# Splitting six of the twelve matmuls of zeros at the head of a matmul-and-rotation kernel

## Chip, cores and metric

The kernel runs on one core of a Trainium2 chip. The metric is the device time of one execution in microseconds (us), as the median of several runs.

## The reference

`x` is 16 x 512 x 768, `weight` 768 x 768, `cos` and `sin` 512 x 64, all float32; there are 12 heads of 64 columns. The product is rotated in halves of each head:

```
y = np.matmul(x, weight).reshape(batch, seq, n_heads, head_dim)
y1, y2 = y[..., :32], y[..., 32:]
out1 = y1 * cos1 - y2 * sin1
out2 = y2 * cos2 + y1 * sin2
out = np.concatenate([out1, out2], axis=-1)
```

Here `cos1` and `sin1` are the first 32 columns of `cos` and `sin`, `cos2` and `sin2` the last 32, spread over batch and heads.

## The kernel before

The 8192 rows of `x` are cut into 64 tiles of 128 rows, four tiles to a group. A tile is loaded, cast to float16, transposed to bring the contraction onto the partitions, and multiplied with the weight, which is held in float16 in six chunks of 128 x 768 (indices 0 to 5). A product of 128 x 768 goes to six banks of 512 columns in PSUM (`py`). VectorE multiplies each stretch of a bank with cosines and sines (`rope`, line 446), GpSimd adds the two products (line 468), and the results are stored.

All instructions are written through one helper, `do`, which works out from the names read and written what each instruction must wait for, and puts it at the end of its engine's program. The order on each engine is thus the order of the calls.

The head of the program is written out by hand. SyncE issues the loads of tile 0 and 1, weight chunk 0, tile 2, weight chunks 1 and 2, tile 3, weight chunks 3 to 5, and then cosines and sines. VectorE first fills `cold` (128 x 512, float16) with zeros. TensorE's program begins with twelve matmuls of `cold` with itself, written by `warm`: nine (`warm(9)`), then the transposes of tile 0, then three more (`warm(3)`), then the transposes of tile 1. Each takes a load of 128 x 128 and streams 512 columns into one of the six banks in turn. The last six open the accumulation of the banks of group 0 with zeros, so that the true matmuls of that group (`mm0`) all add; the first six write zeros that these replace. Nothing waits for any of the twelve by a signal of its own (`tick=False`), but TensorE works in order.

After these come, in TensorE's order, chunk 0 with tiles 0 and 1 (line 340), the transposes of tile 2 (line 260), chunks 1 and 2 with tiles 0 and 1, then tile 2 with chunks 0 and 1, the transposes of tile 3, and so on through chunk 5; each chunk waits for its cast on VectorE (`cast_w`, line 194), and each transpose for the cast of its tile on ScalarE (`castx`, line 194). The transposed tiles 0 and 1 are copied out of PSUM by VectorE, ahead of the cast of chunk 0; later tiles are copied by ScalarE. When chunk 5 is cast, VectorE prepares the sines (lines 625 and 627) and starts on the products. From there on the work is a loop over tiles, with TensorE's matmuls in halves of 64 rows (line 365).

Of the kernel before, what the change touches and what calls it, by code (L numbers as in the profile page):

```python
# [16 lines left out]
class Flow:  # L17
# [24 lines left out]
    def do(self, e, make, reads=(), writes=(), dma=None, tick=True, after=0):  # L42
        need = {}
        for k in reads:
            for s, v in self.wrote.get(k, {}).items():
                need[s] = max(need.get(s, 0), v)
        for k in writes:
            for d in (self.wrote, self.readby):
                for s, v in d.get(k, {}).items():
                    need[s] = max(need.get(s, 0), v)  # L50
        if e == "pe":
            need.pop("pe", None)
            if after:
                need["pe"] = after
        waits = self.settle(e, need)
        for s, v in waits[:-1]:
            self.eng[e].wait_ge(self.sem(s), v)  # L57
        i = make(self.eng[e])
        if waits:
            s, v = waits[-1]  # L60
            i.wait_op(self.sem(s), v, "sem-ge")
        name, step = (dma, 16) if dma else (e, 1)
        self.sem(name)
        self.order[name] = len(self.order) + sum(self.count.values())
        at = self.count[name] + step
        if tick or dma:
            i.then_inc(self.sems[name], step)
            self.count[name] = at
            self.known[name, at] = dict(self.seen[e])
        for k in reads:  # L70
            d = self.readby.setdefault(k, {})
            d[name] = max(d.get(name, 0), at)
        for k in writes:
            self.wrote[k] = {name: at}
            self.readby[k] = {}
        return i
# [32 lines left out]
def kernel(  # L109
# [11 lines left out]
    f = Flow(nc, tc)  # L121
    do = f.do
    P = nc.NUM_PARTITIONS
# [25 lines left out]
    def sbuf(name, shape, dt):  # L149
        return nc.alloc_sbuf_tensor(name, shape, dt).ap()  # L150
# [4 lines left out]
    cold = sbuf("cold", [P, 512], FP16)  # L155
# [26 lines left out]
    py = nc.alloc_psum_tensor("py", [P, 6 * 512], FP32).ap()  # L182
# [322 lines left out]
    def store_half(g, h, c, at):  # L505
# [20 lines left out]
       reads=["ident"], writes=["ident32"])  # L526
# [49 lines left out]
    WARM = 12  # L576
    warmed = [0]

    def warm(k):
        for _ in range(k):  # L580
            b = warmed[0] % 6
            do("pe", lambda eng: eng.matmul(  # L582
                py[:, ts(b, 512)], cold[:, 0:P], cold, start=True, stop=warmed[0] < WARM - 6),
                reads=["cold"], writes=[f"ps{b}"], tick=False)
            warmed[0] += 1

    def mm0(i, c):
# [10 lines left out]

    U0 = units(0)
    warm(9)  # L600
    castx(0, "act")
    turn(0, "dve")
    castx(1, "act")
    warm(3)
    turn(1, "dve")
    castx(2, "act")
# [13 lines left out]
    for c in CHUNKS[3:5]:  # L620
# [8 lines left out]
        reads=["sin", "csn1", "cos"], writes=["csn"])  # L629
# [74 lines left out]
    for i in range(QB, NTILE):  # L704
# [17 lines left out]
        for n, p in enumerate(pieces(g, s)) if i >= ROWS else ():  # L722
# [3 lines left out]
            for c in CHUNKS:  # L726
                mm_piece(i, p, c, c == CHUNKS[0], c == CHUNKS[-1],
                         tick=c == CHUNKS[-1])
# [60 lines left out]
```

## Time and profile before

| | |
|---|---|
| three plain runs | 149.9, 150.1, 150.23 us; median 150.1 us |
| the profiled execution | 150.49 us, with a span of 148.6 us |
| TensorE matmuls (PE) | 140.1 us busy (94%), 1894 |
| TensorE weight loads (PEld) | 110.8 us (75%), 1894 |
| VectorE (DVE) | 127.6 us (86%) |
| ScalarE (ACT) | 75.9 us (51%) |
| GpSimd (POOL) | 123.4 us (83%) |
| the twelve matmuls of zeros (line 582) | 4.4 us busy, all before 6.4 us |

The profile is of one execution, and its times count from the start of the span. A record of a matmul lasts until its result is written, so records of neighbouring matmuls overlap; the pace is read from the distance of their starts. A weight load is a record of its own (PEld) and may run beside a matmul. The chain that ended last is followed back from the last instruction to what released each step.

### The profile page before, as it was taken

How to read it: one execution, taken by the hardware profiler on the slowest of the kernel's cores; microseconds unless marked ns; L12 is line 12 of the kernel's file. 1: busy time of each engine (PE TensorE's matmuls, PEld its weight loads, DVE VectorE, ACT ScalarE, POOL GpSimd, SP SyncE). 2: the span in 40 equal slices, each digit the busy share in tenths (PEclk: the TensorE clock that was granted, in tenths of full speed). 3: DMA queues.
4: the chain of work that ended last, by engine and by line, in shares of the span. 5: the costliest groups of instructions: out<-in, count | busy, mean ns of one | idle time of the engine just before them, and what ended most of it. 6: DMA issues, size and time to landing. Idle time of an engine off the chain costs nothing.

```text
span 148.6 us, 4352 instructions
## 1 busy us (share of the span) xinstructions
PE 140.1 (94%) x1894; PEld 110.8 (75%) x1894; DVE 127.6 (86%) x103; ACT 75.9 (51%) x87; POOL 123.4 (83%) x76
## 2 busy tenths in 40 slices
PE   6769999999999999999999999999999999999960
PEld 2325568888888888888888888888888888766850
DVE  0344998888989999999989998999989999999990
ACT  3444698888242924466262824465455839840010
POOL 2000389999999999999999999779899999899970
PEclk9999999999999999999999999999999999999998
DMA  4999999999999999999999999999999999998783
GB/s 127 352 395 405 400 402 272 249 330 329 331 331 328 333 329 332 342 392 332 327 339 394 360 329 331 382 391 395 391 399 405 396 398 392 400 406 354 275 314 116
DMA packets 36227, 51.28 MB, mean 345 GB/s; under 512 B 7664, under 2 KB 28912, under 8 KB 36208
## 3 DMA queue, kind: packets, MB, share of 16 engines
q1 hardware_dynamic: 16336, 28.05, 54.7%
q10 hardware_dynamic: 14432, 20.97, 38.2%
q0 software_dynamic: 5440, 1.97, 10.7%
q8 instruction: 15, 0.25, 0.6%
q14 instruction: 4, 0.03, 0.1%
HBM read 27.79 MB, written 25.17 MB: 356 GB/s over the span
## 4 chain that ended last, share of the span: by engine, by line
PE 77%; DVE 12%; DMA 5%; issue 2%; SPq 1%; DVEq 0%
PE py L365 68%; DVE tq L446 7%; DMA w_raw<-in_weight_dram 5%; PE py L340 4%; PE pt L275 4%; DVE w_raw L446 2%; SPq L214 1%; PE pt L260 1%; SPq L236 1%; DVE ov L415 1%; DVE py L408 0%; DVE xs L408 0%; DVE w_sb L194 0%; DVEq L57 0%; SPq L784 0%
## 5 line engine op out<-in xcount | busy, mean ns | idle before, releaser
L468 POOL TENSOR_TENSOR ov<-tq 128x512 f32<-128x512 f32 (+3 forms) x34 | 76.1, 2261 | 19.5 <-DVE tq L446 19.0
L446 DVE TENSOR_TENSOR tq<-py,csn 128x1024 f32<-128x1024 f32 (+2 forms) x51 | 74.4, 1495 | 3.8 <-PE py L365 2.9
L365 PE MATMUL py<-w_sb,xt 64*128 64x512 f16 (+1 forms) x768 | 73.8, 323 | 0.0
L365 PEld LDWEIGHTS py<-w_sb,xt 64*128 64x128 f16 x768 | 53.5, 94 | 10.6 <-DVE tq L446 0.4
L365 PE MATMUL py<-w_sb,xp 64*128 64x256 f16 (+1 forms) x528 | 52.1, 323 | 0.0
L194 ACT COPY xt<-pt 128x768 f16<-128x768 f16 x38 | 30.3, 801 | 38.6 <-PE pt L275 33.9
L194 ACT CAST xc<-xs 128x768 f16<-128x768 f32 x40 | 36.1, 907 | 18.8 <-PE py L365 7.4
L365 PEld LDWEIGHTS py<-w_sb,xp 64*128 64x128 f16 x528 | 37.1, 94 | 6.6
L446 DVE TENSOR_TENSOR w_raw<-py,csn 128x1024 f32<-128x1024 f32 (+1 forms) x22 | 35.3, 1604 | 2.8 <-PE py L365 2.4
L468 POOL TENSOR_TENSOR ov<-w_raw 128x1536 f32<-128x1536 f32 (+2 forms) x15 | 35.5, 2379 | 0.5 <-DVE w_raw L446 0.4
L340 PE MATMUL py<-w_sb,xt 128*128 128x256 f16 (+1 forms) x102 | 17.0, 317 | 1.6 <-DVE w_sb L194 1.3
L340 PEld LDWEIGHTS py<-w_sb,xt 128*128 128x128 f16 x102 | 9.2, 98 | 7.7 <-DVE w_sb L194 3.0
L275 PEld LDWEIGHTS pt<-ident,xc 64*128 64x128 f16 x408 | 13.2, 95 | 1.3 <-issue 0.2
L275 PE MATMUL pt<-ident,xc 64*128 64x64 f16 x408 | 13.0, 191 | 0.0
L229 POOL DMA_DIRECT2D xh<-in_x_dram x20 | 11.7, 592 | 0.0
L194 ACT CAST xd<-xb 128x1536 f16<-128x1536 f32 x7 | 11.5, 1637 | 0.0
L194 DVE CAST w_sb<-w_raw 128x768 f16<-128x768 f32 x6 | 3.4, 560 | 4.1 <-DMA w_raw<-in_weight_dram 4.0
L303 DVE STREAM_TRANSPOSE xp<-xd 128x768 f32<-128x768 f32 x7 | 6.8, 970 | 0.0
L303 DVE STREAM_TRANSPOSE xp<-xh 128x768 f32<-128x768 f32 x5 | 6.2, 1242 | 0.0
L582 PE MATMUL py<-cold 128*128 128x512 f16 x12 | 4.4, 525 | 1.4 <-DVE cold L519 1.4
L194 ACT COPY ov<-py 128x256 f32<-128x256 f32 x1 | 0.4, 372 | 10.0 <-PE py L478 10.0
L194 DVE COPY xt<-pt 128x768 f16<-128x768 f16 x2 | 1.1, 557 | 4.8 <-PE pt L260 4.8
(26 smaller groups left out, 22.6 us busy)
## 6 DMA issues: line engine op xcount, KB each, us to landing
out_dram<-ov ACTq DMA_DIRECT2D x53, 384.0 KB, 12.6
xs<-in_x_dram SPq DMA_DIRECT2D x40, 384.0 KB, 14.1
xb<-in_x_dram SPq DMA_DIRECT2D x28, 192.0 KB, 16.2
out_dram<-ov SPq DMA_DIRECT2D x4, 768.0 KB, 6.1
w_raw<-in_weight_dram SPq DMA_DIRECT2D x6, 384.0 KB, 7.5
xh<-in_x_dram POOLq DMA_DIRECT2D x20, 96.0 KB, 13.1
out_dram<-ov SPq DMA_DIRECT2D x1, 384.0 KB, 3.7
out_dram<-ov SPq DMA_DIRECT2D x3, 128.0 KB, 2.6
```

What stands on the lines that cost most here:

```text
L194: eng.copy(out=o, in_=i_) if e == "act" else eng.tensor_copy(out=o, in_=i_)
L214: do(e, lambda eng: eng.dma_start(out=xs_b[k], in_=x[b].rearrange("(p r) h -> r p h", r=SB)[r]), writes=[f"xs{k}"], dma=f"xs{k}")
L229: do(e, lambda eng: eng.dma_start(out=dst[ts(q, R)], in_=src[r, q]), writes=[f"{name}q{q}"], dma=name)
L236: do(e, lambda eng: eng.dma_start(out=w_raw[:, t, h], in_=wv[t, h]), writes=[f"wr{t}{h}"], dma=f"ov{t}_{1536 * (1 - h)}")
L260: do("pe", lambda eng: eng.transpose(pt[:, t, h, :], src[:, t, h, :], ident), reads=[f"xc{c}", "ident"], writes=[f"pt{k}"], tick=(t, h) == ...
L275: do("pe", lambda eng: eng.transpose(pts[r][:, t, h, :], src[rows, t, h, :], ident[rows, rows]), reads=[f"xc{c}", "ident"], writes=[f"pt{r ...
L303: do("dve", lambda eng: eng.transpose(out=dst, in_=src), reads=rd, writes=[f"xp{z}"])
L340: do("pe", lambda eng: eng.matmul(ps, get(t, h), w_sb[:, t, h, a - s * H : z - s * H], start=start, stop=stop), reads=[key, f"w{t}{h}"], w ...
L365: do("pe", lambda eng: eng.matmul(py[:, a:z], get(t, h)[rows], w_sb[rows, t, h, a - s * H : z - s * H], start=start, stop=not opens and en ...
L446: do("dve", lambda eng: eng.tensor_tensor(out=tq.rearrange("p j (h d) -> p j h d", d=D), in0=ps.rearrange("p (h d) -> p h d", d=D) .unsque ...
L468: do(adder, lambda eng: eng.tensor_tensor(out=ov_b[o][:, ds(c0, w)].rearrange("p (h t d) -> p h t d", t=2, d=HD), in0=tq[:, 0].rearrange(" ...
L582: do("pe", lambda eng: eng.matmul(py[:, ts(b, 512)], cold[:, 0:P], cold, start=True, stop=warmed[0] < WARM - 6), reads=["cold"], writes=[f ...
```

## The change

Of the twelve matmuls of zeros, the first six are each written as four: the same load of 128 x 128 zeros, and 128 columns streamed instead of 512, into the four quarters of the same bank. The last six stay as they are, and so does everything else. Since each matmul has its load, TensorE's program has 18 loads and 18 matmuls more.

```diff
     def warm(k):
         for _ in range(k):
             b = warmed[0] % 6
-            do("pe", lambda eng: eng.matmul(
-                py[:, ts(b, 512)], cold[:, 0:P], cold, start=True, stop=warmed[0] < WARM - 6),
-                reads=["cold"], writes=[f"ps{b}"], tick=False)
+            n = 128 if warmed[0] < WARM - 6 else 512
+            for c in range(0, 512, n):
+                do("pe", lambda eng: eng.matmul(
+                    py[:, ds(b * 512 + c, n)], cold[:, 0:P], cold[:, ds(c, n)],
+                    start=True, stop=warmed[0] < WARM - 6),
+                    reads=["cold"], writes=[f"ps{b}"], tick=False)
             warmed[0] += 1
```

## The prediction

> **What bounds the kernel now.** I read the page first, then the chain that ended last in order of time, then the timeline of the first 20 us, because the edit touches only TensorE's first instructions. The page gives the span and who carries the end:
>
> ```profile
> span 148.6 us, 4352 instructions
> ...
> ## 4 chain that ended last, share of the span: by engine, by line
> PE 77%; DVE 12%; DMA 5%; issue 2%; SPq 1%; DVEq 0%
> ```
>
> Three quarters of the chain is TensorE (PE), so an edit on TensorE could matter. But the share is an average; the question is where that chain enters TensorE. In order of time it does so here:
>
> ```profile
> 3.28 6.97 DMA w_raw<-in_weight_dram
> 10.25 0.02 issue
> 10.27 0.57 DVE w_sb L194
> 10.84 0.05 issue
> 10.89 1.47 PE py L340 x8
> ...
> 123.72 1.95 PE py L365 x17
> ```
>
> Before 10.89 us nothing on TensorE is on the chain. The end is set by the third chunk of the weight (index 2): its transfer takes 6.97 us from 3.28 and lands at 10.25, VectorE (DVE) casts it in 0.57 us, and only then does TensorE start a stretch that the chain follows nearly without a break to 125 us. The twelve matmuls of zeros lie wholly ahead of it. The timeline shows how they lie beside the real work (columns: start, duration, engine, line and operation; in brackets the idle time before and what ended it):
>
> ```profile
> 1.40 3.57 PE L582 MATMUL py<-cold 128*128 128x512 f16 x9 [1.40 <-DVE cold L519]
> 1.80 0.15 PEld L582 LDWEIGHTS py<-cold 128*128 128x128 f16 x1 [0.28 <-issue]
> ...
> 4.17 1.82 ACT L194 CAST xc<-xs 128x768 f16<-128x768 f32 x2 [1.98 <-DMA xs<-in_x_dram]
> ...
> 4.36 0.12 PEld L582 LDWEIGHTS py<-cold 128*128 128x128 f16 x1 [0.28 <-issue]
> 5.16 0.35 PEld L260 LDWEIGHTS pt<-ident,xc 128*128 128x128 f16 x6 [0.68 <-issue]
> 5.19 0.49 PE L260 MATMUL pt<-ident,xc 128*128 128x128 f16 x6 [0.22 <-ACT xc L194]
> ...
> 5.53 0.81 PE L582 MATMUL py<-cold 128*128 128x512 f16 x3
> 5.73 0.56 DVE L194 COPY xt<-pt 128x768 f16<-128x768 f16 x1 [4.38 <-PE pt L260]
> ...
> 6.17 0.50 PE L260 MATMUL pt<-ident,xc 128*128 128x128 f16 x6
> ...
> 6.71 0.56 DVE L194 COPY xt<-pt 128x768 f16<-128x768 f16 x1 [0.43 <-PE pt L260]
> ...
> 7.38 0.56 DVE L194 CAST w_sb<-w_raw 128x768 f16<-128x768 f32 x1
> ...
> 8.00 0.82 PE L340 MATMUL py<-w_sb,xt 128*128 128x512 f16 x4 [1.33 <-DVE w_sb L194]
> ...
> 9.27 0.51 PE L260 MATMUL pt<-ident,xc 128*128 128x128 f16 x6 [0.45 <-ACT xc L194]
> 9.30 0.56 DVE L194 CAST w_sb<-w_raw 128x768 f16<-128x768 f32 x1 [1.36 <-DMA w_raw<-in_weight_dram]
> ```
>
> Nine matmuls of zeros run from 1.40. Seven loads lie between 1.80 and 4.36 at equal steps, so one matmul of 512 columns takes (4.36 - 1.80)/6 = 0.427 us there. The three that start at 5.53 take 0.81 us together. With the shortest record of one, 0.379 (quoted next), that is (0.81 - 0.38)/2 = 0.215 us a step. TensorE therefore runs at half pace first and at full pace later. The change falls at about 4.38: the nine end at 1.40 + 3.57 = 4.97, less the 0.379 - 0.215 = 0.164 us by which a record outlasts its step, 4.81; the eighth, loaded at 4.36, and the ninth thus fit in 0.45 us, two steps at full pace and 0.02 us. The page's clock row does not show the half pace (its first slice is a 9, as all but the last are), so I go by the steps:
>
> ```profile
> PEclk9999999999999999999999999999999999999998
> ...
> L582 PEld LDWEIGHTS py<-cold x12: 97/132/151, 1.4 to 5.7; 128*128 128x128 f16 x12
> L582 PE MATMUL py<-cold x12: 379/607/635, 1.4 to 6.0; 128*128 128x512 f16 x12
> L260 PEld LDWEIGHTS pt<-ident,xc x36: 96/98/101, 5.2 to 18.1; 128*128 128x128 f16 x36
> L260 PE MATMUL pt<-ident,xc x36: 216/220/232, 5.2 to 18.1; 128*128 128x128 f16 x36
> ```
>
> These are the durations (minimum, median, maximum, in ns) of the zero matmuls and of the transposes. The transposes matter as a price, because their shape is exactly the new one: a load of 128x128 and a stream of 128 columns. Six take 0.50 us from 6.17; less the record of the last (0.22), that is (0.50 - 0.22)/5 = 0.056 us a pair at full pace. That is a quarter of 0.215, although each pair's own load record is 0.098 us: the loads hide behind the streams.
>
> **The change part by part.** It removes six pairs of load and 512-column matmul and adds 24 pairs of load and 128-column matmul: 18 loads and 18 matmuls more, on the same banks, with the same operand of zeros. It adds no wait: the first matmul still waits for the memset of zeros, none of the new ones signals, and the six that open the accumulation in the banks are as before.
>
> *Streaming time.* Columns stay the same: 6 x 512 = 24 x 128. At half pace a 128-column stream is 0.427/4 = 0.107 us, so 24 x 0.107 = 2.56 us against 6 x 0.427 = 2.56 us. Difference: 0.
>
> *The loads.* At half pace one load's record is 0.15 us, longer than the 0.107 us stream meant to hide it, and no row shows a 128-column matmul at half pace. So I bound it. Low end: hidden, as at full pace (0.098 us record, 0.056 us step); cost 0. It cannot be below zero, since the columns are the floor. High end: load and stream strictly one after the other. A pair then takes 0.107 + 0.15 = 0.257 us at half pace and 0.056 + 0.098 = 0.154 us at full pace. Between 1.40 and 4.38 (2.98 us) 11.6 pairs pass; the other 12.4 take 1.91 us, to 6.29; the three long ones end at 6.29 + 3 x 0.215 = 6.94, against 4.81 before. I take the low end, because its row is the same shape and both load and stream slow together.
>
> [...]
>
> *What that reaches.* What covers both ends is the wait for the weight. At the low end the nine end at 4.81 and the first transposes wait for ScalarE's cast until 5.19 anyway. At the high end everything follows in TensorE's order: transposes of tile 0 from 6.94 to 7.28, the last record outlasting its step by 0.16 more; three long matmuls to 7.92; transposes of tile 1 to 8.26, visible at 8.42; VectorE's copy (0.56) to 9.0, its cast of chunk 0 (0.56) to about 9.6; four matmuls of 1536 columns (3 x 0.215 = 0.65) to 10.28; transposes of tile 2 (0.33) to 10.61; chunk 1 (0.65) to 11.26. Chunk 2 then starts at 11.26 instead of 10.89, 0.37 late. What is next behind that?
>
> ```profile
> 14.81 1.74 PEld L340 LDWEIGHTS py<-w_sb,xt 128*128 128x128 f16 x12 [0.22 <-DVE w_sb L194]
> ...
> 15.28 0.23 DVE L627 TENSOR_SCALAR csn<-sin_sb 128x128 f32<-128x128 f32 x1
> 15.54 6.75 DVE L446 TENSOR_TENSOR tq<-py,csn 128x1024 f32<-128x1024 f32 x4
> ...
> 16.84 0.34 PEld L260 LDWEIGHTS pt<-ident,xc 128*128 128x128 f16 x6 [0.30 <-ACT xc L194]
> ...
> 19.30 0.56 PEld L365 LDWEIGHTS py<-w_sb,xt 64*128 64x128 f16 x7 [0.36 <-DVE tq L446]
> ```
>
> The first product on VectorE starts at 15.54, right after its own scaling of the sines. The matmul it needs starts at 14.81 and takes about 0.39, so it is there at 15.20: 0.34 us of slack. A shift of 0.37 moves VectorE by 0.03 us, and TensorE, which waits for VectorE at 19.30 and for ScalarE at 16.84, takes up the rest in those waits. So the sum is 0 at the low end and 0.03 us at the high end.
>
> *The pace.* The doubling at 4.38 could move. Earlier is worth nothing, since 5.19 is ScalarE's. Later: if the pace doubled only after tile 1's transposes, nine long matmuls' worth would end at 5.24, transposes (0.64) at 5.88, three long ones at 7.16, transposes at 7.80, visible at 7.96, copy and cast to 9.13, then at full pace 9.82, 10.15, 10.80: still ahead of 10.89. So up to about 7.8 us a late doubling is free too.
>
> The profiled execution took 150.49 us with its span of 148.6; the three plain runs have a median of 150.1, 0.39 below, from 149.9 to 150.23. A sum of 0 gives 150.49 there and 150.1 as the median. A measurement can tell about 0.2% here, 0.3 us.
>
> **The rivals.**
>
> *Slower: the small matmuls do not bring the pace up.* Suppose that only long matmuls in an unbroken stretch do, 2.98 us of them as before. Then three at 3.96 are followed by transposes at 5.24, three more break off at 7.16, and the next long stretch is chunk 0's, from 9.17. At half pace it takes 3 x 0.427 = 1.28 to 10.45, transposes to 11.09, and with the doubling at 9.17 + 2.98 = 12.15 chunk 1 ends at 12.26. Chunk 2 is 1.37 late, less 0.34 of slack: 1.03 us, which nothing later gives back as the chain stays on TensorE and VectorE; 151.1 us. It decides once chunk 2 starts after 10.89 + 0.34 = 11.23. Against it: the same columns stream without a gap at the low end, and the trace before shows the pace holding through idle time and transposes from 6.5 to 8.0. For it: no row shows the pace rising on short matmuls. [...]
>
> [...]
>
> *Faster: more loads bring the pace up sooner in executions in which it comes late.* The plain runs may differ in that from the profiled one. The gain is then at most what the late ones lose: from the median 150.1 to the fastest, 149.9, or a little below if all three lost something. Against it: a late doubling is free up to 7.8 us.
>
> **How the numbers follow.** No change gets 0.68, of which 0.02 strays over 0.2% on either side by scatter; the first slower rival 0.10 (151.1), the second 0.06 (151.4); the faster one 0.16 (149.9), half of it beyond 0.2%. Faster is 0.08 + 0.02 = 0.10, slower 0.10 + 0.06 + 0.02 = 0.18, the same 0.64 + 0.08 = 0.72. The forecast is 150.1. The plain runs spread over 0.33 us, so half of that, some 0.16, is what another set may stray. The range is the fastest run less that, 149.75, which takes in the faster rival, and the slowest plus that, the 0.03 us of the loads and a little of the rivals, 150.5; both slower rivals, 0.16 together, stay outside.
>
> **What would show it.** Right: 24 zero matmuls starting 0.107 us apart from 1.40, the nine old ones' place ending near 4.8, tile 0's transposes near 5.19 waiting for ScalarE, chunk 0 at 8.00, the chain entering TensorE near 10.89 from the weight's transfer. The load step is wrong if the starts are further apart than 0.107; that costs the end nothing unless chunk 2 slips past 11.23. The forecast is wrong if matmuls of 512 columns still step by 0.427 after 7.8 us, or if the chain enters TensorE through line 582.

## The result, and the profile after

The changed kernel took 149.81 us (median of 17 runs, 149.07 to 150.56) against 150.22 us (17 runs, 149.70 to 150.65). The ratio is 0.9961, with a 95% interval of 0.9944 to 0.9978: 0.39% faster, 0.22% to 0.56%. "The same" was forecast, at 150.1 us in a range from 149.75 to 150.5; the time lies in the range, but the gain is real and had been given 1 in 10. Ratios here leave out executions more than 1.5% above the fastest of their kernel, and they are not the ratio of the two medians, which differ here by 0.41 us (0.27%).

The head looks as forecast. The page's span and the chain in order of time, of after:

```profile
span 148.2 us, 4388 instructions
...
3.28 6.84 DMA w_raw<-in_weight_dram
10.12 0.02 issue
10.14 0.57 DVE w_sb L194
10.72 0.05 issue
10.76 1.47 PE py L340 x8
```

The chain still enters TensorE from the third weight chunk, 0.13 us earlier than before because the transfer took 6.84 us instead of 6.97. The timeline of after:

```profile
1.40 2.69 PEld L584 LDWEIGHTS py<-cold 128*128 128x128 f16 x26 [1.40 <-DVE cold L519]
1.40 4.02 PE L584 MATMUL py<-cold 128*128 128x128 f16 x27 [1.40 <-DVE cold L519]
...
5.29 0.80 PE L260 MATMUL pt<-ident,xc 128*128 128x128 f16 x6
5.88 1.10 PE L584 MATMUL py<-cold 128*128 128x512 f16 x3
...
7.83 0.55 DVE L194 CAST w_sb<-w_raw 128x768 f16<-128x768 f32 x1
```

The single starts in the trace (1.697, 1.804, 1.911 and so on) are 0.107 us apart, so the loads hide behind the streams at half pace too. TensorE doubled its pace later in this execution, about 6.5 us instead of 4.4: the transposes of tile 0 take 0.80 us here, 0.49 before. Chunk 0 is cast 0.45 us later and nothing follows from it.

So the gain of the profiled pair, 0.4 us of span, is not at the head. Nor is it in the long middle: VectorE's first product starts 0.15 us earlier (15.39 against 15.54), but that lead is lost at about 125 us (more on this below), and its last add ends within 0.07 us of before. The two rows are of the last add before and after:

```profile
144.13 0.42 DVE L415 TENSOR_TENSOR ov<-py,xs 128x256 f32<-128x256 f32 x1
```

```profile
144.19 0.42 DVE L415 TENSOR_TENSOR ov<-py,xs 128x256 f32<-128x256 f32 x1
```

It lies behind that: the last stores. Transfers from 139 to 149 us, first before, then after (queue, packets, MB, share; and per issue the size and the time from issue to landing):

```profile
q8 instruction: 1, 0.02, 0.5%
issues: line engine op xcount, KB each, median us to landing
out_dram<-ov SPq DMA_DIRECT2D x1, 384.0 KB, 3.7
out_dram<-ov ACTq DMA_DIRECT2D x1, 384.0 KB, 3.4
out_dram<-ov SPq DMA_DIRECT2D x3, 128.0 KB, 2.6
```

```profile
q10 hardware_dynamic: 288, 0.52, 14.0%
issues: line engine op xcount, KB each, median us to landing
out_dram<-ov SPq DMA_DIRECT2D x1, 384.0 KB, 2.3
out_dram<-ov ACTq DMA_DIRECT2D x1, 384.0 KB, 2.4
out_dram<-ov SPq DMA_DIRECT2D x3, 128.0 KB, 2.0
```

Before, one packet of the queue named "instruction" falls among the last stores, and all of them land later. After, there is none (the list of queues ends with q10). The last two half microseconds show what goes with it, before and after (the two columns at the end are the DMA share and GB/s):

```profile
146.00:146.50 0.50, 0.00 (x0) 0.00 (x0) 0.00 (x0) 0.00 (x0) 0.00 (x0) 1.00 0.61 203
146.50:147.00 0.50, 0.00 (x0) 0.00 (x0) 0.00 (x0) 0.00 (x0) 0.00 (x0) 1.00 0.05 16
```

```profile
146.00:146.50 0.50, 0.00 (x0) 0.00 (x0) 0.00 (x0) 0.00 (x0) 0.00 (x0) 0.91 0.70 230
146.50:147.00 0.50, 0.00 (x0) 0.00 (x0) 0.00 (x0) 0.00 (x0) 0.00 (x0) 0.50 0.00 0
```

A share of 0.05 is less than one engine of sixteen: a single DMA engine works on alone, and the end waits for it. The packets of the trace say the same: before, the last eight of 1,024 bytes start about 0.042 us apart, one behind the other with nothing beside them, and the last packet of all ends at 146.88.

I take the instruction packet for a fetch of TensorE's program. The page of before, like that of after, has the row

```profile
q8 instruction: 15, 0.25, 0.6%
```

By the trace these are 15 packets of 16,384 bytes each, for 3788 loads and matmuls; between two of them TensorE starts on average 246 loads and matmuls. The last packet starts at 141.69 us before (it is 0.88 us long) and at 137.96 after. Of the loads and matmuls, 3763 have started by then before and 3729 after. That is 34 fewer, and 36 of the 3729 are the new ones, so in the work that both kernels share the last fetch comes 70 records earlier. That the new ones moved it is what the experiments test; why by 70 and not by 36 stays open.

From this two theories. **A:** the gain comes because 36 more instructions ahead of the end move TensorE's last program fetch out of the last stores. **B:** the head did it, by short columns, more loads or the pace. What A speaks of is read within one execution: the time from the end of VectorE's last add to the end of the last store's packet, 2.33 us before and 1.84 after, is called the last stretch below.

### The profile page after: what moved, and what is told of

Same layout as the page of the kernel before. It is cut to its first block, busy times and chain, and to the rows that moved or that the text cites. A ratio compares the mean times of both kernels' runs of the same rounds, so it can differ in the third digit from the quotient of the medians.

```text
span 148.2 us, 4388 instructions
## 1 busy us (share of the span) xinstructions
PE 140.9 (95%) x1912; PEld 113.0 (76%) x1912; DVE 127.5 (86%) x103; ACT 75.9 (51%) x87; POOL 123.3 (83%) x76
## 4 chain that ended last, share of the span: by engine, by line
PE 77%; DVE 12%; DMA 5%; issue 2%; SPq 1%; DVEq 0%
PE py L365 68%; DVE tq L446 7%; DMA w_raw<-in_weight_dram 5%; PE py L340 5%; PE pt L275 4%; DVE w_raw L446 2%; SPq L214 1%; PE pt L260 1%; SPq L236 1%; DVE ov L415 1%; DVE py L408 0%; DVE xs L408 0%; DVE w_sb L194 0%; DVEq L57 0%; SPq L787 0%
## 5 line engine op out<-in xcount | busy, mean ns | idle before, releaser
L584 PE MATMUL py<-cold 128*128 128x128 f16 (+1 forms) x30 | 5.1, 363 | 1.4 <-DVE cold L519 1.4
```

The lines of the kernel that those rows point to most:

```text
L584: do("pe", lambda eng: eng.matmul(py[:, ds(b * 512 + c, n)], cold[:, 0:P], cold[:, ds(c, n)], start=True, stop=warmed[0] < WARM - 6), read ...
```

## The experiments

All but e9 and e12 are edits of the kernel before. A wait on a semaphore that is long met changes nothing in what is computed; two of them make one instruction (the trace of e1 has 36 more semaphore records on TensorE for its 72 waits, 53 against 17).

**e1, 36 instructions more at the head.**

```diff
     turn(1, "dve")
+    for _ in range(72):
+        nc.tensor.wait_ge(f.sem("dve"), 1)
```

> The kernel before, with its twelve zero matmuls of 512 columns, and 72 waits on an already met semaphore in TensorE's program behind the transposes of tile 1; two such waits make one instruction, so 36 instructions more, as many as the change added. Theory A (program fetch: 36 more instructions move the last 16 KB fetch of TensorE's program out of the last stores): that fetch starts near 138 us instead of 141.7, the last 384 KB store of SyncE lands in about 2.3 us instead of 3.7, and the time is 0.3 to 0.5 us below the kernel before. Theory B (short columns or more weight loads at the head, the pace of TensorE): no gain, within 0.15 us of before, fetch anywhere.

Measured: the last stretch was 1.82 us, as A says, but the time was 152.22 us, with a ratio of 1.0086 (1.0049 to 1.0123). The waits were dear, about 0.09 us an instruction (3.26 us over 36). The timeline of e1:

```profile
6.26 0.50 PE L260 MATMUL pt<-ident,xc 128*128 128x128 f16 x6
10.02 0.81 PE L340 MATMUL py<-w_sb,xt 128*128 128x512 f16 x4 [3.26 <-issue]
```

TensorE stood still for 3.26 us and began chunk 0 two microseconds late. The longest runs had the lowest granted clock (0.977 to 0.989, against 0.997 and 0.998 in the three shortest). The profiled execution, 150.83 us, is one of those three. The expected gain was missed, so e5 repeats the idea without waits.

**e2, the same at the end.** The 72 waits stand behind `for add in after_all + late: add()`.

> The kernel before, with the same 36 instructions more (72 met waits) behind the last matmul of TensorE's program instead of at its head. Theory A: what comes before the last fetch is not longer, so it stays near 141.7 us inside the last stores, and the time is within 0.15 us of before. If it were the sheer length of the program, wherever it is added, the gain of 0.4 us would be here too. Theory B: within 0.15 us of before.

Measured: the last fetch came at 142.09 us, the last stretch was 2.50 us, and the ratio 0.999 (0.9962 to 1.0017). The length of the program alone brings no gain that can be told.

**e3 and e4, one block more, and one block and 36.**

```diff
     for i in range(QB, NTILE):
         g, s = divmod(i, QB)
+        if 8 <= i < 56:
+            for _ in range(2 * ((i - 7) * spread // 48 - (i - 8) * spread // 48)):
+                nc.tensor.wait_ge(f.sem("dve"), 1)
```

with `spread` 256 in e3 and 292 in e4.

> The kernel before with 256 instructions more (512 met waits) spread evenly over the tiles 8 to 55: just one 16 KB block of TensorE's program (64 bytes each). Theory A: one fetch more in all (16), and the last again near 141.7 us inside the last stores: store landing about 3.7 us as before. If the waits are hidden by TensorE's queue the time is that of before, within 0.15 us; if not, it is longer by their cost, which the next kernel shares. Theory B says nothing of the fetch; no gain.

> The same with 292 instructions more (584 met waits), one block and 36. Theory A: the last fetch is again near 138 us, ahead of the last stores, which land in about 2.3 us; 0.3 to 0.5 us less than the kernel with 256 more. Theory B: no difference between the two but the cost of 36 waits, so the same or slower.

Measured: e3 has one fetch more, by its page:

```profile
q8 instruction: 16, 0.26, 0.6%
```

So the packets are TensorE's: 256 instructions added to its program bring one more. The last comes 2.94 us ahead of the end of VectorE's last add (2.86 before), and the last stretch is 2.24 us. By that a packet of 16,384 bytes holds about 256 instructions, some 64 bytes each; ahead of this run only the 246 loads and matmuls between two packets of before spoke for it. In e4 it comes 6.80 us ahead (6.66 in the change), and the last stretch is 1.84. That repeats, one block on, what A asks of the fetch and of the stretch. The times do not: 152.47 us (ratio 1.0140, 1.0110 to 1.0169) and 154.35 us (1.0259, 1.0230 to 1.0289). A had asked for 0.3 to 0.5 us less in e4 than in e3, and it took 1.9 us more, as theory B allows. The waits are not hidden, and the last 36 cost more than the tail gives, so these two say nothing for A on the total.

**e5, the change's 36 instructions as zeros elsewhere.**

```diff
     turn(1, "dve")
+    for j in range(18):
+        do("pe", lambda eng: eng.matmul(
+            py[:, ds(j % 6 * 512, 128)], cold[:, 0:P], cold[:, 0:128], start=False, stop=False),
+            reads=["cold"], writes=[f"ps{j % 6}"], tick=False)
```

> The kernel before with its twelve zero matmuls whole, and 18 more of 128 columns (18 loads and 18 matmuls, the change's 36 instructions) behind the transposes of tile 1, where TensorE has 1.3 us to wait; they add zeros to open banks. 18 x 0.056 = 1.0 us fits into that wait. Theory A (36 instructions more move TensorE's last program fetch ahead of the last stores): fetch near 138 to 139 us, the stretch from VectorE's last add to the last store's packet 1.8 us instead of 2.3, time 0.4 us below before, as with the change. Theory B (the head: short columns in place of long, or the pace): no gain, within 0.15 us.

Measured: the time was 149.91 us, with a ratio of 0.9960 (0.9933 to 0.9988); the last fetch came at 137.62, and the last stretch was 1.83. The transfers of e5, again from 139 to 149 us:

```profile
q10 hardware_dynamic: 288, 0.52, 14.1%
issues: line engine op xcount, KB each, median us to landing
out_dram<-ov SPq DMA_DIRECT2D x1, 384.0 KB, 2.3
```

There is no instruction packet, and the store lands in 2.3 us. The gain is there with all twelve zero matmuls whole and in their places, and although the pace doubled only at 7.2 us. So short columns in place of long ones and an earlier pace fall as the cause. More loads at the head, the third part of B, e5 has as well; e9 below bears on them.

**e6, short but not split.**

```diff
-                py[:, ts(b, 512)], cold[:, 0:P], cold, start=True, stop=warmed[0] < WARM - 6),
+                py[:, ds(b * 512, n)], cold[:, 0:P], cold[:, 0:n], start=True, stop=warmed[0] < WARM - 6),
```

with `n` as in the change.

> The first six zero matmuls stream 128 columns instead of 512 and are not split: no instruction more, and three quarters of their columns left out. Theory A: last fetch at 141.7 to 142.1 us, last stretch 2.3 to 2.5 us, time as before within 0.15 us. Theory B, short columns as such: 0.4 us faster, last stretch anywhere.

Measured: the last stretch was 2.49 us, as A says; but the time was 152.18 us, with a ratio of 1.0081 (1.0039 to 1.0122). Neither theory expected that. Two of the twelve executions took 150.24 and 150.65 us, the others 152.02 to 153.02; the profiled one took 153.0. The timeline of e6:

```profile
9.42 1.46 PE L340 MATMUL py<-w_sb,xt 128*128 128x512 f16 x4 [1.12 <-DVE w_sb L194]
10.68 0.85 PE L260 MATMUL pt<-ident,xc 128*128 128x128 f16 x6
11.32 3.65 PE L340 MATMUL py<-w_sb,xt 128*128 128x512 f16 x12
14.80 0.50 PE L260 MATMUL pt<-ident,xc 128*128 128x128 f16 x6
```

Four matmuls take 1.46 us (0.82 before) and twelve 3.65 us (2.44): TensorE stays at half pace to about 14.4 us. With three quarters of the first columns gone the pace does not rise in time in this execution, and the first product on VectorE starts at 17.90 instead of 15.54.

**e7, nine zeros instead of 18** (18 instructions more).

> Nine more zero matmuls of 128 columns behind the transposes of tile 1 instead of 18, so 18 instructions more. Theory A: the last fetch comes between, at 139 to 141 us, and the last stretch is between 1.8 and 2.3 us; time 0.1 to 0.4 us below before. Theory B: as before.

Measured: the time was 149.89 us, with a ratio of 0.9965 (0.9936 to 0.9994); the last fetch came at 139.08, and the last stretch was 1.83. Within the intervals, half the instructions give the same gain.

**e8, without the six:** `warmed[0] = 6` and `warm(3)` in place of `warm(9)`.

> The first six zero matmuls are left out: 12 instructions fewer. The pace may rise a little later, which the wait for the weight covers. Theory A: the last fetch comes later than 141.7, at about 142 to 143 us, still inside the last stores; the last stretch is 2.3 us or more, time as before or up to 0.4 us slower. Theory B: without the six the head can only be slower; no statement on the end.

Measured: the time was 152.64 us, with a ratio of 1.0121 (1.0078 to 1.0164), and the last stretch 2.06 us. The pace rises only at 13.5 us, late as in e6; I had expected the wait for the weight to cover a later rise. The fetch came at 143.85, 3.14 us ahead of the last add, where A had asked for less than the 2.86 of before: with 12 instructions fewer it moved 0.28 us further ahead instead of closer. The stretch, under the 2.3 us expected, follows the fetch, but where the fetch falls A did not foresee here.

**e9 and e10, the split with one block more, and e3 again.** e9 is the changed kernel with the spread waits of e3 and `spread` 220, so 256 instructions more in all.

> The changed kernel (six zero matmuls split, 36 instructions) and 220 instructions more (440 met waits) spread over tiles 8 to 55: 256 in all, one block of TensorE's program, as in the kernel with 256 waits' worth and no split. Theory A: 16 fetches, the last again 2.7 to 3.2 us ahead of VectorE's last add, the last stretch 2.0 to 2.5 us and no longer 1.84, so the split brings nothing here: the same time as the unsplit kernel with 256 more within 0.5 us (it has 36 waits' cost less). Theory B: the split is faster than that kernel by 0.4 us or more and the last stretch has nothing to do with it.

> The unsplit kernel with 256 instructions more, again, for comparison with the split one on the same chip. Both theories: about 152.5 us, 1.4% above before; theory A: last stretch 2.2 to 2.5 us.

Measured: the last stretch was 2.42 us in e9 and 2.39 in e10. The transfers of e9, again from 139 to 149 us:

```profile
q8 instruction: 1, 0.02, 0.6%
...
out_dram<-ov SPq DMA_DIRECT2D x1, 384.0 KB, 3.8
```

With the split in place and the fetch back among the last stores, the long landing is back: the split by itself, its loads included, does not shorten the tail. The times are 151.29 us (ratio 1.0060, 1.0037 to 1.0083) and 152.63 us (1.0159, 1.0131 to 1.0187), further apart than expected. VectorE's last add already ends 1.21 us earlier in e9, at 145.51 against 146.72, and its first product does not (15.51 against 15.41), so the difference arises in the middle, where e9 has 220 costly instructions and e10 256. Theory B had forecast e9 ahead by 0.4 us or more. The 36 waits that e9 lacks may be enough, as the 36 between e3 and e4 cost 1.9 us, but no run shows it. On the split's own share of the total these two decide nothing.

**e11, three zeros** (6 instructions more).

> Three more zero matmuls of 128 columns behind the transposes of tile 1: 6 instructions more. So far the last stretch shrank by about 1 us for each us by which the fetch came earlier, from 2.50 us at 2.73 us ahead of VectorE's last add to 2.06 at 3.14. Theory A: 6 instructions of about 0.054 us move the fetch from 2.86 to about 3.2 us ahead of that add, and the last stretch is 1.9 to 2.1 us, between before and the change. Theory B: the stretch stays at 2.3.

Measured: the fetch came at 140.84, 4.06 us ahead of the last add, and the last stretch was 2.20 us. That is less than before and more than the change, but the expected step of 1 us per us was wrong. The one execution took 150.59 us, which says nothing on the time.

**e12, the change again.**

> The changed kernel again, on this chip and day. Theory A: last fetch near 138 us, last stretch 1.8 us, 0.3 to 0.6 us below before. Theory B: the same time, with no statement on the stretch.

Measured: the time was 150.11 us against 150.34, with a ratio of 0.9980 (0.9958 to 1.0001); the last stretch was 1.83 us and the fetch came at 138.77. The gain is smaller, and its interval takes in no gain at all; it overlaps with the first.

All executions with a profile, in order of the fetch's lead (from the fetch's start to the end of VectorE's last add):

```
kernel        instructions more   last fetch  lead   last stretch (us)
              ahead of the end
e2            0                   142.09      2.73   2.50
e6            0                   144.29      2.74   2.49
e9            256 (split)         142.70      2.81   2.42
e10           256                 143.87      2.85   2.39
before        0                   141.69      2.86   2.33
e3            256                 143.73      2.94   2.24
e8            -12                 143.85      3.14   2.06
e11           6                   140.84      4.06   2.20
e7            18                  139.08      5.42   1.83
e1            36                  139.26      6.17   1.82
after         36 (split)          137.96      6.66   1.84
e12           36 (split)          138.77      6.67   1.83
e4            292                 141.07      6.80   1.84
e5            36                  137.62      6.82   1.83
```

With a lead of 5.4 us or more the last stretch is 1.82 to 1.84 us in all six executions. With less it is 2.06 to 2.50. The difference is the engine that works on alone: at the end of those six, fewer than four packets are on their way for 0.03 to 0.05 us, and at the end of the other eight for 0.26 to 0.72. Without that piece the last stretch is 1.78 to 1.82 us in all fourteen.

## Why the prediction was wrong

*The steps that held.* The 128-column matmuls stepped by 0.107 us; the head stayed covered by the weight's transfer; chunk 0 at 8.44 instead of 8.00 cost nothing; the chain entered TensorE at 10.76.

*The step that failed.* Under "the change part by part" I counted 18 loads and 18 matmuls more and priced them only where they run; what they do to the fetches of the program I put at nothing, without a reason. By the traces of before and after, all 15 fetches of TensorE's program start earlier, by 0.51 to 4.31 us, and the last one, 3.73 us earlier, is out of the last stores. The page had the row, 15 packets named instruction, and I left it out; no rival had this cause. It is worth 0.49 us in the last stretch of the profiled pair (2.33 less 1.84), against 0.59 us of the ratio (0.84 to 0.33) and 0.30 us in e12 (0.63 to none). So it is large enough for the gain, and e5 and e7 show that it comes without the split. That the time still lay in the range was luck: the range had been widened for the scatter and for a faster rival, and neither was the cause.

*A second effect, the other way.* Where VectorE transposes the operand `xd` near 125 us (up to 128 in the slower kernels), it may have to wait for ScalarE's cast of it. The rows are of before, after and e12:

```profile
124.87 0.98 DVE L303 STREAM_TRANSPOSE xp<-xd 128x768 f32<-128x768 f32 x1
```

```profile
124.93 0.98 DVE L303 STREAM_TRANSPOSE xp<-xd 128x768 f32<-128x768 f32 x1 [0.17 <-ACT xd L194]
```

```profile
125.76 0.98 DVE L303 STREAM_TRANSPOSE xp<-xd 128x768 f32<-128x768 f32 x1 [0.69 <-ACT xd L194]
```

In the seven kernels of the table with a lead of 4.06 us or more, this wait is 0.17 to 0.69 us; in the other seven it is at most 0.07. So the loss goes with the moved fetches and takes back part of what they give; that they cause it, and by holding up which transfer, was not tried. The profiled pair adds up with it: 0.12 us gained up to there, 0.18 lost there and 0.49 gained in the last stretch make 0.43, the 0.4 us of the spans.

*The rivals.* The pace doubled at about 6.5 us in after, behind 24 short matmuls and with no more than 1.3 us of long ones in a stretch, so the first slower rival did not come. Nor did the second (0.06, 151.4 us): no run shows the late doubling from loads in series that this term stands for, and in after the loads hid at 0.107 us a step. The faster rival had the right sign and the wrong cause: the pace doubled later in the profiled execution of after, not sooner.

*The pace.* That a late doubling is free held as far as the runs go (e5 doubled at 7.2 us and has a ratio of 0.9960, e12 at 7.4 and 0.9980, the times by the trace); between there and the 7.8 us of the estimate none lies. What I did not see is how much the columns of zeros matter: with fewer it came at 14.4 us in e6 and 13.5 in e8, and the ratios are 1.0081 and 1.0121.

*What stays open.* Why e12 gained less than the first comparison: in its profiled execution, the longest of its twelve, VectorE's last add ends 0.82 us later than in after. Of that, 0.31 is there at the first product, and the rest is the longer wait for the cast of `xd`. Such a wait goes with moved fetches; why it is 0.17 us in one execution of this kernel and 0.69 in another is open. It is also open why the last fetch moved by more records than were added, and the wrong way in e8, and whether the split has a small effect of its own: e9 and e10 could not tell. No version tried is faster than the change beyond the intervals; e7 has the same gain with half as many instructions.

## What to carry to other kernels

Here TensorE's program came in by DMA while it ran, in 15 packets of 16,384 bytes between 22.8 and 141.7 us of before (16 packets in e3, with 256 instructions more). With 18 and 36 instructions more ahead of the end, the last fetch came at 139.08 us (e7) and 137.96 (after) instead of 141.69. Look in the window of the last stores for a packet of the instruction queue and for a last half microsecond in which one engine of sixteen works alone. And before crediting a small gain to the place of an edit, put as many instructions of another kind elsewhere and see whether it stays.

## What the runs showed of the hardware

Each of the 15 fetches of 16,384 bytes was one packet, of 0.88 to 1.08 us in before and 0.89 to 1.28 in after. With one among the last stores the last stretch was up to 0.67 us longer (2.50 us in e2 against 1.83 in e5, e7 and e12). Already met waits on TensorE were not free in e1: 36 such instructions in a row held it for 3.26 us.
